# Decoder trunk on one core: products of the convolution in pairs of slots, three kinds of rows read from PSUM, softmax weights scaled on ScalarE and mixed a product later

## The chip, the core and the metric

One core of a Trainium2 chip runs the whole trunk for 256 tokens. The metric is the device time of one execution in microseconds (us), median of three runs: 2081.55 us before (2081.02 to 2082.35). Matrix products run on TensorE (PE), element work on VectorE (DVE), ScalarE (ACT) and GpSimd (POOL); SyncE (SP) issues the loads.

## The reference, cut to what matters

```python
# layer 0: Conformer convolution, then MLP.  layer 1: attention, then MLP.  D = 2048, 256 tokens
u = rmsnorm(h) @ w_in + b_in;  a, gate = split(u);  u = a * sigmoid(gate)
u = causal depthwise conv(u, 31 taps) + b_dw
h = h + silu(layernorm(u)) @ w_out + b_out
h = h + relu(rmsnorm(h) @ m_in)**2 @ m_out          # 2048 -> 8192 -> 2048
k, v = split(rmsnorm(h) @ w_kv)                     # 4 key heads; k rotated in 32 of 128 dims
q = rotate(rmsnorm(h) @ w_q)                        # 16 heads
o = softmax mixture of three dilated windows        # 256 keys: one mask of counts, added as logs
h = h + o @ w_o;  h = h + MLP as above;  out = rmsnorm(h)
```

## The kernel before, in words

Tokens lie along the free dimension (256 columns), features along the partitions, so h is 16 tiles of 128x256. Every weight tile is 128x2048 (1 MB, 16 blocks of 128 contraction rows), loaded in the order of use, and split in two: ACT rounds it to `hi` (line 138), DVE or, for the tiles listed in `POOL_LO`, POOL subtracts `lo = raw - hi` (line 140). Activations are split the same way. `product` (lines 189 to 195) makes two matmuls for each block: `hi` times the 512 columns of both parts, and `lo` times the 256 columns of the first. `product3` (208 to 210) makes three matmuls of 256 columns instead, all adding into the same 256 columns, so that no half is left to be joined. `joined` (199, 200) adds the two halves that `product` leaves.

Stage 1, the convolution layer, goes over 16 channel tiles c. Each has two products (`pa`, `pg`; eight of the 32 tiles are multiplied unsplit by line 214), then a sigmoid and the gated `u` (411, 412), then `conv`: of the 31 taps ACT writes 11, and after POOL has added pairs of them three more, into slots of `prod` buffers (318, 326); DVE does the other 17 taps itself (339 to 344) and sums the slots with two reductions over eight and six slots (350). A slot is 256 adjacent numbers, so the reduction reads numbers that lie 1024 bytes apart. Tile 15 gives 18 of its taps to PE as products with diagonal matrices (309). PE adds up a provisional mean over the first ten tiles (433), which is copied to `shift` in SBUF (436); DVE subtracts it from every tile (`center`, 376), ACT squares, PE sums columns (236). From these come the LayerNorm's factor and offset, spread over all partitions in PSUM (247) and copied to SBUF (459). DVE applies them (475, 476), ACT applies silu (478), and `split_into` (220, 221) makes the operand of the next product. `project` starts with four weight tiles at once (16 blocks in `steps`), so PE can begin with the first of these operands.

After the MLP come k and v, then 16 query products, two heads to a pair p. `rotate` (576 to 579) shuffles 32 partitions into `sh` and mixes them with the tables `ropes`. `scores` makes the scaled and masked scores, the maximum, the exponentials with their sums (648), the reciprocals (650) and the scaled weights (653). `flip` transposes them on PE (663 to 666), `mix` multiplies by v (678, 679). The order by program: after the product of an even head `scores(p-1)` and `mix(p-2)`, after an odd one `flip(p-1)`; the last of them stand among the first blocks of the projection by w_o. The scheduler that builds the program draws each engine's order ahead of time from this order and from its own estimate of times; at run time each engine goes through its list in order.

At the end line 721 multiplies the 16 tiles of h by the row of the final norm, and five transfers store them.

Of the kernel before, what the change touches and what calls it, by code (L numbers as in the profile page):

```python
# [18 lines left out]
P = 128  # L19
# [28 lines left out]
POOL_LO = (set(range(36)) - {28}) | set(range(183, 202, 2))  # L48
# [13 lines left out]
def decoder_kernel(ctx, tc, xT, vec, rope, mask, w_in, w_out, w_k, w_v, w_q, w_o, m_in, m_out, out):  # L62
# [220 lines left out]
    with ExitStack() as s1:  # L283
# [16 lines left out]
        def conv(c, u):  # L300
# [13 lines left out]

            def scaled(buf, slots):
                nonlocal j
                for i in slots:
                    nc.scalar.activation(out=buf[:, i, :], in_=u[:, j:j + T], func=AF.Copy, scale=tap(c, j))  # L318
                    j += 1

            for n, m in pieces:
                buf = prodp.tile([P, SLOTS, T], F32, name="prod")
                scaled(buf, range(carry, carry + n))
                if m:
                    room = slice(carry + m, carry + 2 * m)
                    nc.gpsimd.tensor_tensor(out=buf[:, carry:carry + m, :], in0=buf[:, carry:carry + m, :],
                                            in1=buf[:, room, :], op=ALU.add)
                    refills.append((buf, range(SLOTS)[room]))
# [6 lines left out]
            for i, j in enumerate(range(j, TAPS)):  # L335
# [7 lines left out]
                else:  # L343
                    nc.vector.scalar_tensor_tensor(out=a if j < TAPS - 2 else last[:, i % 2, :], in0=x,  # L344
# [3 lines left out]
            for i, (buf, n) in enumerate(bufs):  # L348
                dst = bufs[i + 1][0][:, 0, :] if i + 1 < len(bufs) else v_of(c)
                nc.vector.tensor_reduce(out=dst, in_=buf[:, :n, :].rearrange("p j t -> p t j"), axis=AX.X, op=ALU.add)  # L350
# [40 lines left out]
        for c in range(KT):  # L391
# [38 lines left out]
            if 2 <= c <= SHIFT + 1:  # L430
                if pmean is None:
                    pmean = ps_tile()
                nc.tensor.matmul(pmean[:, :T], lhsT=ones_d, rhs=v_of(c - 2), start=c == 2, stop=c == SHIFT + 1)
            if c == SHIFT + 1:
                shift = up.tile([P, T], F32, name="shift")
                nc.scalar.activation(out=shift, in_=pmean[:, :T], func=AF.Copy, scale=KT / SHIFT)
# [19 lines left out]
        norm = act_tile(F32)  # L456
        norm_ps = pb.rearrange("p (i t) -> p i t", i=2)
        for i in range(2):
            nc.scalar.copy(out=norm[:, i, :], in_=pb[:, i * T:(i + 1) * T])
# [12 lines left out]
    for c in range(KT):  # L472
        z = tmp()
        n = norm if c else norm_ps
        nc.vector.tensor_tensor(out=z, in0=v_of(c), in1=n[:, 0, :], op=ALU.mult)
        nc.vector.tensor_tensor(out=z, in0=z, in1=n[:, 1, :], op=ALU.add)
        s = tmp()
# [95 lines left out]
    def rotate(src):  # L573

        sh = tp.tile([ROT, T], F32, name="sh", tag="t")
        nc.vector.stream_shuffle(sh, src[0:ROT, :], [(i + ROT // 2) % ROT for i in range(ROT)])
        nc.vector.tensor_tensor(out=sh, in0=sh, in1=ropes[:, 1, :], op=ALU.mult)  # L577
        nc.vector.tensor_tensor(out=src[0:ROT, :], in0=src[0:ROT, :], in1=ropes[:, 0, :], op=ALU.mult)
        nc.vector.tensor_tensor(out=src[0:ROT, :], in0=src[0:ROT, :], in1=sh, op=ALU.add)
# [6 lines left out]
    for g in range(NKV):  # L586
# [5 lines left out]
        else:  # L592
            if rb is None:
                rb = rms_kv.rows()
            while waiting:
# [3 lines left out]
                rotate(ks[:, i, :])  # L599
# [27 lines left out]
    def scores(p):  # L627
# [7 lines left out]
        for b in (1, 0):  # L635
# [15 lines left out]
            for j in range(2):  # L651
                i = 2 * b + j
                nc.vector.tensor_scalar(out=pr[:, j, :n], in0=pr[:, j, :n], scalar1=rl[:, i:i + 1], scalar2=None,
                                        op0=ALU.mult)
# [30 lines left out]
    for i in range(NH):  # L685
# [4 lines left out]
        product(ps, take(), acts, range(KT))  # L690
        q = q_of[p][:, i % 2, :]
        joined(q, ps)
        rotate(q)
        if i % 2 == 0:
            if p >= 1:
                scores(p - 1)
            if p >= 2:
                mix(p - 2)
        elif p >= 1:
            flip(p - 1)  # L700
# [3 lines left out]
    for k, do in ((11, lambda: mix(NP - 1)), (7, lambda: flip(NP - 1)), (4, lambda: mix(NP - 2)), (2, lambda: scores(NP - 1))):  # L704
# [82 lines left out]
```

## Time and profile before

| | |
|---|---|
| median of 3 runs | 2081.55 us |
| the profiled execution, its own time | 2082.01 us |
| span of its instructions | 2080.2 us |
| PE busy, loads of weights | 2016.3 us (97%), 1776.2 us |
| DVE, ACT, POOL busy | 1354.6, 979.7, 212.9 us |
| stage 1 (first matmul of the projection by w_out) | ends at 268.84 us |
| attention (first scores to the MLP) | about 1142 to 1283 us |

A span is read from the span's start. Matmuls are pipelined and their ends are modelled, so PE counts as busy for some 0.2 us after it could have begun the next; its work is better read from the distance between starts. A time in brackets behind a row is the idle time just before it and what ended it.

### The profile page before, as it was taken

The page shows a single profiled execution, that of the slowest core. Times are in us where ns is not written, and L with a number is a line of the kernel's source. Part 1 is how long each engine was busy: PE and PEld are TensorE (multiplying, and loading weights), DVE is VectorE, ACT ScalarE, POOL GpSimd, SP SyncE. Part 2 cuts the span into 40 slices and gives each one's busy share as a digit, 9 for nine tenths or more (in the row PEclk, how much of TensorE's full clock was granted, in tenths as well). Part 3 has the DMA queues.
Part 4 walks back from the last instruction along what each step waited for, and adds up shares of the span by engine and source line. Part 5 has one row for each costly group of instructions (what it writes and reads, how often), then busy time and mean ns, then how long its engine had stood idle before and what let it go on. Part 6 is the DMA issues. An engine that isn't in the chain of part 4 may idle for free.

```text
span 2080.2 us, 28137 instructions
## 1 busy us (share of the span) xinstructions
PE 2016.3 (97%) x11702; PEld 1776.2 (85%) x11702; DVE 1354.6 (65%) x1807; ACT 979.7 (47%) x1324; POOL 212.9 (10%) x83
## 2 busy tenths in 40 slices
PE   8989889999999999999999899999999999999997
PEld 7888778888888888888888787888888888888886
DVE  7999977556556556555676786755555555655664
ACT  4676664443453354345454444444345335434442
POOL 2687600000000000000003220000000000000000
PEclk9999899999999999999999999999999999999999
DMA  7344325555555555555555334555555555555552
GB/s 290 130 154 159 105 108 185 187 185 193 187 196 184 185 194 186 186 191 193 182 183 186 122 138 142 191 188 184 187 192 192 182 189 195 183 186 196 185 185 78
DMA packets 51583, 367.39 MB, mean 177 GB/s; under 512 B 5856, under 2 KB 5856, under 8 KB 7552
## 3 DMA queue, kind: packets, MB, share of 16 engines
q1 hardware_dynamic: 51312, 365.60, 50.7%
q8 instruction: 91, 1.49, 0.3%
q14 instruction: 36, 0.29, 0.0%
q10 hardware_dynamic: 144, 0.01, 0.0%
HBM read 363.49 MB, written 2.10 MB: 176 GB/s over the span
## 4 chain that ended last, share of the span: by engine, by line
PE 50%; issue 35%; DVE 12%; ACT 2%; POOL 0%; DVEq 0%; POOLq 0%; ACTq 0%
PE ps L194 31%; PE ps L195 16%; DVE ps L344 3%; DVE prod L350 2%; DVE act L350 2%; DVE sh L577 1%; ACT hi L138 1%; ACT prod L318 1%; DVE prod L344 1%; DVE act L376 0%; PE ps L639 0%; DVE act L221 0%; PE ps L612 0%; PE ps L611 0%; PE ps L610 0%
## 5 line engine op out<-in xcount | busy, mean ns | idle before, releaser
L194 PE MATMUL ps<-act,hi 128*128 128x512 f32 x4928 | 1731.3, 395 | 4.9 <-DVE act L221 4.1
L195 PE MATMUL ps<-act,lo 128*128 128x256 f32 x4928 | 1381.7, 281 | 4.1 <-DVE lo L140 4.1
L194 PEld LDWEIGHTS ps<-act,hi 128*128 128x128 f32 x4928 | 925.1, 188 | 217.7 <-DVE act L221 4.8
L138 ACT CAST hi<-raw 128x2048 fp32r<-128x2048 f32 x336 | 641.0, 1910 | 853.5 <-PE ps L194 691.4
L140 DVE TENSOR_TENSOR lo<-raw,hi 128x2048 fp32r<-128x2048 f32 x298 | 682.9, 2291 | 431.6 <-ACT hi L138 428.6
L195 PEld LDWEIGHTS ps<-act,lo 128*128 128x128 f32 x4928 | 933.3, 189 | 6.6 <-DVE lo L140 4.7
L494 DVE TENSOR_TENSOR h<-ps,h 128x256 f32<-128x256 f32 x288 | 119.6, 424 | 193.4 <-PE ps L195 189.2
L140 POOL TENSOR_TENSOR lo<-raw,hi 128x2048 fp32r<-128x2048 f32 x38 | 175.0, 4608 | 129.7 <-ACT hi L138 103.6
L241 POOL TENSOR_TENSOR rc<-ms,neg_half 128x2 f32<-128x2 f32 x5 | 3.6, 730 | 1666.3 <-DVE ms L270 1666.3
L318 ACT ACTIVATE prod<-u,vecs 128x256 f32<-128x256 f32 x217 | 90.5, 497 | 58.1 <-DVE u L412 53.8
L208 PE MATMUL ps<-act,hi 128*128 128x256 f32 x384 | 113.1, 294 | 0.0
L210 PE MATMUL ps<-act,lo 128*128 128x256 f32 x384 | 111.1, 289 | 0.1
L209 PE MATMUL ps<-act,hi 128*128 128x256 f32 x384 | 110.9, 289 | 0.0
L344 DVE SCALAR_TENSOR_TENSOR ps<-u,vecs,ps 128x256 f32<-128x256 f32 x197 | 79.6, 483 | 0.0
L208 PEld LDWEIGHTS ps<-act,hi 128*128 128x128 f32 x384 | 76.0, 198 | 0.3
L209 PEld LDWEIGHTS ps<-act,hi 128*128 128x128 f32 x384 | 76.0, 198 | 0.3
L210 PEld LDWEIGHTS ps<-act,lo 128*128 128x128 f32 x384 | 75.9, 198 | 0.3 <-POOL lo L140 0.3
L536 ACT ACTIVATE t<-t 128x256 f32<-128x256 f32 x128 | 52.5, 410 | 42.5 <-DVE t L534 42.5
L221 DVE TENSOR_TENSOR act<-t,act 128x256 fp32r<-128x256 f32 x144 | 60.1, 417 | 8.3 <-ACT act L220 8.3
L214 PE MATMUL ps<-act,raw 128*128 128x256 f32 x256 | 57.8, 386 | 6.7 <-DMA raw<-in_w_in 6.7
L214 PEld LDWEIGHTS ps<-act,raw 128*128 128x128 f32 x256 | 49.2, 194 | 13.4 <-DVE act L295 6.7
L350 DVE TENSOR_REDUCE prod<-prod 128x256 f32<-128x2048 f32 x15 | 58.2, 3877 | 1.6 <-ACT prod L318 0.5
(113 smaller groups left out, 903.0 us busy)
## 6 DMA issues: line engine op xcount, KB each, us to landing
raw<-in_m_in SPq DMA_DIRECT2D x128, 1024.0 KB, 4.8
raw<-in_m_out SPq DMA_DIRECT2D x128, 1024.0 KB, 4.8
raw<-in_w_in SPq DMA_DIRECT2D x31, 1024.0 KB, 4.9
raw<-in_w_out SPq DMA_DIRECT2D x16, 1024.0 KB, 4.9
raw<-in_w_q SPq DMA_DIRECT2D x16, 1024.0 KB, 4.8
raw<-in_w_o SPq DMA_DIRECT2D x16, 1024.0 KB, 4.9
raw<-in_w_k SPq DMA_DIRECT2D x4, 1024.0 KB, 4.9
raw<-in_w_v SPq DMA_DIRECT2D x4, 1024.0 KB, 4.8
```

The lines of the kernel that those rows point to most:

```text
L138: nc.scalar.copy(out=hi, in_=raw)
L140: eng.tensor_tensor(out=lo, in0=raw, in1=hi.bitcast(F32), op=ALU.subtract)
L194: nc.tensor.matmul(ps, lhsT=wh, rhs=a.rearrange("p i t -> p (i t)"), start=k == 0, stop=False)
L195: nc.tensor.matmul(ps[:, :T], lhsT=wl, rhs=a[:, 0, :], start=False, stop=k == KT - 1)
L208: nc.tensor.matmul(ps, lhsT=wh, rhs=a[:, 0, :], start=k == 0, stop=False)
L209: nc.tensor.matmul(ps, lhsT=wh, rhs=a[:, 1, :], start=False, stop=False)
L210: nc.tensor.matmul(ps, lhsT=wl, rhs=a[:, 0, :], start=False, stop=k == KT - 1)
L214: nc.tensor.matmul(ps, lhsT=w[:, k * P:(k + 1) * P], rhs=act_of(k), start=k == 0, stop=k == KT - 1)
L318: nc.scalar.activation(out=buf[:, i, :], in_=u[:, j:j + T], func=AF.Copy, scale=tap(c, j))
L344: nc.vector.scalar_tensor_tensor(out=a if j < TAPS - 2 else last[:, i % 2, :], in0=x, scalar=tap(c, j), in1=a, op0=ALU.mult, op1=ALU.add)
L350: nc.vector.tensor_reduce(out=dst, in_=buf[:, :n, :].rearrange("p j t -> p t j"), axis=AX.X, op=ALU.add)
L494: nc.vector.tensor_tensor(out=h[:, f, :], in0=half, in1=h[:, f, :], op=ALU.add)
```

## The change

Six edits. (1) The buffers `prod` hold slots in pairs: number t of slots 2j and 2j+1 lie side by side, 8 bytes from one t to the next. ACT, POOL and DVE write and read single slots at that step (POOL's addition of two pairs becomes two instructions), and the reduction runs over pairs. (2) The provisional mean's matrix of ones holds the final factor, and `center` reads the mean from PSUM; the copy 436 is gone. (3) The LayerNorm rows are read from PSUM by all 16 tiles; the two copies 459 are gone; silu writes to PSUM. (4) `rotate` keeps `sh` in PSUM and takes a source and a destination; queries are made by `product3`, copied by ACT and rotated from PSUM, so that `joined` is gone there. (5) The softmax weights are scaled by ACT, not DVE; `flip` and `mix` of a pair come one product later each. (6) Three more `lo` tiles (36 to 38, of w_out) go from DVE to POOL, and the last multiplication is done in 5 wide instructions, not 16.

```diff
-POOL_LO = (set(range(36)) - {28}) | set(range(183, 202, 2))
+POOL_LO = (set(range(39)) - {28}) | set(range(183, 202, 2))
+        ones_s = up.tile([P, P], F32, name="ones_s")
+        nc.gpsimd.memset(ones_s, 1.0 / (SHIFT * P))
...
+            def slot(buf, i):
+                return buf[:, i // 2, :, i % 2]
...
-                    nc.scalar.activation(out=buf[:, i, :], in_=u[:, j:j + T], func=AF.Copy, scale=tap(c, j))
+                    nc.scalar.activation(out=slot(buf, i), in_=u[:, j:j + T], func=AF.Copy, scale=tap(c, j))
...
-                buf = prodp.tile([P, SLOTS, T], F32, name="prod")
+                buf = prodp.tile([P, SLOTS // 2, T, 2], F32, name="prod")
...
-                    nc.gpsimd.tensor_tensor(out=buf[:, carry:carry + m, :], in0=buf[:, carry:carry + m, :],
-                                            in1=buf[:, room, :], op=ALU.add)
+                    for i in range(carry, carry + m):
+                        nc.gpsimd.tensor_tensor(out=slot(buf, i), in0=slot(buf, i), in1=slot(buf, i + m), op=ALU.add)
...
-                nc.vector.tensor_reduce(out=dst, in_=buf[:, :n, :].rearrange("p j t -> p t j"), axis=AX.X, op=ALU.add)
+                nc.vector.tensor_reduce(out=dst, in_=buf[:, :n // 2].rearrange("p j t i -> p t j i"), axis=AX.XY,
+                                        op=ALU.add)
...
-                nc.tensor.matmul(pmean[:, :T], lhsT=ones_d, rhs=v_of(c - 2), start=c == 2, stop=c == SHIFT + 1)
+                nc.tensor.matmul(pmean[:, :T], lhsT=ones_s, rhs=v_of(c - 2), start=c == 2, stop=c == SHIFT + 1)
             if c == SHIFT + 1:
-                shift = up.tile([P, T], F32, name="shift")
-                nc.scalar.activation(out=shift, in_=pmean[:, :T], func=AF.Copy, scale=KT / SHIFT)
+                shift = pmean[:, :T]
...
-        norm = act_tile(F32)
-        norm_ps = pb.rearrange("p (i t) -> p i t", i=2)
-        for i in range(2):
-            nc.scalar.copy(out=norm[:, i, :], in_=pb[:, i * T:(i + 1) * T])
+        norm = pb.rearrange("p (i t) -> p i t", i=2)
...
-        s = tmp()
+        s = ps_tile()[:, :T]
         nc.scalar.activation(out=s, in_=z, func=AF.Silu, scale=col("lng", c), bias=col("lnb", c))
...
-    def rotate(src):
-        sh = tp.tile([ROT, T], F32, name="sh", tag="t")
+    def rotate(dst, src):
+        sh = ps_tile()[:ROT, :T]
         nc.vector.stream_shuffle(sh, src[0:ROT, :], [(i + ROT // 2) % ROT for i in range(ROT)])
         nc.vector.tensor_tensor(out=sh, in0=sh, in1=ropes[:, 1, :], op=ALU.mult)
-        nc.vector.tensor_tensor(out=src[0:ROT, :], in0=src[0:ROT, :], in1=ropes[:, 0, :], op=ALU.mult)
-        nc.vector.tensor_tensor(out=src[0:ROT, :], in0=src[0:ROT, :], in1=sh, op=ALU.add)
+        nc.vector.tensor_tensor(out=dst[0:ROT, :], in0=src[0:ROT, :], in1=ropes[:, 0, :], op=ALU.mult)
+        nc.vector.tensor_tensor(out=dst[0:ROT, :], in0=sh, in1=dst[0:ROT, :], op=ALU.add)
...
-                nc.vector.tensor_scalar(out=pr[:, j, :n], in0=pr[:, j, :n], scalar1=rl[:, i:i + 1], scalar2=None,
-                                        op0=ALU.mult)
+                nc.scalar.activation(out=pr[:, j, :n], in_=pr[:, j, :n], func=AF.Copy, scale=rl[:, i:i + 1])
...
-        product(ps, take(), acts, range(KT))
+        product3(ps[:, :T], take(), acts, range(KT))
         q = q_of[p][:, i % 2, :]
-        joined(q, ps)
-        rotate(q)
+        nc.scalar.copy(out=q, in_=ps[:, :T])
+        rotate(q, ps[:, :T])
         if i % 2 == 0:
+            if p >= 2:
+                flip(p - 2)
             if p >= 1:
                 scores(p - 1)
-            if p >= 2:
-                mix(p - 2)
-        elif p >= 1:
-            flip(p - 1)
+        elif p >= 2:
+            mix(p - 2)
...
-    for k, do in ((11, lambda: mix(NP - 1)), (7, lambda: flip(NP - 1)), (4, lambda: mix(NP - 2)), (2, lambda: scores(NP - 1))):
+    for k, do in ((12, lambda: mix(NP - 1)), (9, lambda: flip(NP - 1)), (5, lambda: mix(NP - 2)),
+                  (2, lambda: flip(NP - 2)), (1, lambda: scores(NP - 1))):
...
-        for i in range(f, f + n):
-            nc.vector.tensor_tensor(out=h[:, i, :], in0=h[:, i, :], in1=rb, op=ALU.mult)
+        nc.vector.tensor_tensor(out=h[:, f:f + n, :], in0=h[:, f:f + n, :],
+                                in1=rb.unsqueeze(1).broadcast_to([P, n, T]), op=ALU.mult)
```

## Rows read from the trace of the kernel before

**Rows 1.** Page, part 1: busy us, share of the span, instructions.

```profile
PE 2016.3 (97%) x11702; PEld 1776.2 (85%) x11702; DVE 1354.6 (65%) x1807; ACT 979.7 (47%) x1324; POOL 212.9 (10%) x83
```

**Rows 2.** Waits of PE, whole span: line, releaser, us in total, times, longest.

```profile
PE ps L433 <- DVE act L350: 13.1, 8, 2.8
PE ps L663 <- DVE act L653: 8.0, 2, 7.4
...
PE ps L236 <- ACT t L378: 6.4, 3, 3.4
PE ps L195 <- DVE lo L140: 4.1, 2, 2.3
...
PE ps L236 <- DVE act L376: 3.3, 2, 2.7
PE ps L639 <- DVE act L579: 3.0, 4, 0.8
```

**Rows 3.** Windows: us; busy PE, PEld, DVE, ACT, POOL (instructions); granted clock; DMA.

```profile
220.00:240.00 20.00, 17.84 (x119) 17.64 (x119) 20.00 (x28) 13.13 (x26) 13.60 (x6) 0.80 0.31 106
240.00:260.00 20.00, 17.30 (x77) 15.44 (x77) 20.00 (x27) 11.36 (x24) 9.36 (x4) 0.74 0.31 106
1140.00:1160.00 20.00, 12.63 (x66) 10.83 (x65) 14.79 (x26) 7.49 (x13) 7.59 (x2) 0.83 0.46 157
```

**Rows 4.** Timeline of PE over one steady channel: start, length, line, shapes, wait.

```profile
122.01 0.70 PE L433 MATMUL ps<-act,ones_d 128*128 128x256 f32 x2 [1.71 <-DVE act L350]
...
133.82 0.28 PE L209 MATMUL ps<-act,hi 128*128 128x256 f32 x1
133.94 0.28 PE L210 MATMUL ps<-act,lo 128*128 128x256 f32 x1
135.93 0.70 PE L433 MATMUL ps<-act,ones_d 128*128 128x256 f32 x2 [1.71 <-DVE act L350]
```

**Rows 5.** Groups of DVE, 0 to 300 us: shapes, count, busy us, mean ns, idle.

```profile
L350 DVE TENSOR_REDUCE prod<-prod 128x256 f32<-128x2048 f32 x15 | 58.2, 3877 | 1.6 <-ACT prod L318 0.5
L350 DVE TENSOR_REDUCE act<-prod 128x256 f32<-128x1536 f32 x15 | 43.4, 2896 | 0.4
...
L376 DVE TENSOR_TENSOR act<-act,shift 128x256 f32<-128x256 f32 x16 | 9.9, 661 | 0.0
```

**Rows 6.** Groups of DVE in the attention, 1140 to 1290 us.

```profile
L577 DVE TENSOR_TENSOR sh<-sh,ropes 32x256 f32<-32x256 f32 x15 | 27.6, 1843 | 0.3
...
L645 DVE TENSOR_REDUCE mx<-act 128x2 f32<-128x512 f32 x8 | 5.3, 669 | 0.0
...
L645 DVE TENSOR_REDUCE mx<-act 128x2 f32<-128x256 f32 x8 | 3.2, 402 | 0.0
```

**Rows 7.** Groups: POOL from 0 to 300 us, and line 140 on DVE (page, part 5).

```profile
L140 POOL TENSOR_TENSOR lo<-raw,hi 128x2048 fp32r<-128x2048 f32 x28 | 129.1, 4613 | 23.3 <-ACT hi L138 8.1 <-DVE ps L344 6.2 <-issue 4.7
...
L326 POOL TENSOR_TENSOR prod<-prod 128x256 f32<-128x256 f32 x16 | 14.0, 873 | 31.7 <-ACT prod L318 19.5 <-DVE ps L342 8.4 <-DVE act L376 3.8
...
L140 DVE TENSOR_TENSOR lo<-raw,hi 128x2048 fp32r<-128x2048 f32 x298 | 682.9, 2291 | 431.6 <-ACT hi L138 428.6
```

**Rows 8.** Timeline of PE at the end of stage 1.

```profile
241.49 0.28 PE L210 MATMUL ps<-act,lo 128*128 128x256 f32 x1
...
249.98 10.63 PE L309 MATMUL ps<-u,act 128*128 128x256 f32 x36
...
268.84 0.80 PE L194 MATMUL ps<-act,hi 128*128 128x512 f32 x1 [3.18 <-DVE act L221]
```

**Rows 9.** Groups of ACT, 262 to 270 us.

```profile
L459 ACT COPY act<-ps 128x256 f32<-128x256 f32 x2 | 0.6, 374 | 2.8 <-PE ps L247 2.8
```

**Rows 10.** Timeline of PE inside a product of 512 and 256 columns.

```profile
1251.06 0.39 PE L194 MATMUL ps<-act,hi 128*128 128x512 f32 x1
...
1251.41 0.39 PE L194 MATMUL ps<-act,hi 128*128 128x512 f32 x1
```

**Rows 11.** Groups of DVE, 2060 us to the end.

```profile
L721 DVE TENSOR_TENSOR h<-h,t 128x256 f32<-128x256 f32 x16 | 5.5, 421 | 1.7 <-ACT t L279 1.7
```

More of the change, by code (lines that the diff above doesn't have):

```diff
@@ L343, in conv @@
                 else:
-                    nc.vector.scalar_tensor_tensor(out=a if j < TAPS - 2 else last[:, i % 2, :], in0=x,
+                    nc.vector.scalar_tensor_tensor(out=a if j < TAPS - 2 else slot(last, i % 2), in0=x,
                                                    scalar=tap(c, j), in1=a, op0=ALU.mult, op1=ALU.add)
@@ L348, in conv @@
             for i, (buf, n) in enumerate(bufs):
-                dst = bufs[i + 1][0][:, 0, :] if i + 1 < len(bufs) else v_of(c)
-                nc.vector.tensor_reduce(out=dst, in_=buf[:, :n, :].rearrange("p j t -> p t j"), axis=AX.X, op=ALU.add)
+                dst = slot(bufs[i + 1][0], 0) if i + 1 < len(bufs) else v_of(c)
+                nc.vector.tensor_reduce(out=dst, in_=buf[:, :n // 2].rearrange("p j t i -> p t j i"), axis=AX.XY,
+                                        op=ALU.add)
             if n_pe:
@@ L473, in decoder_kernel @@
         z = tmp()
-        n = norm if c else norm_ps
-        nc.vector.tensor_tensor(out=z, in0=v_of(c), in1=n[:, 0, :], op=ALU.mult)
-        nc.vector.tensor_tensor(out=z, in0=z, in1=n[:, 1, :], op=ALU.add)
-        s = tmp()
+        nc.vector.tensor_tensor(out=z, in0=v_of(c), in1=norm[:, 0, :], op=ALU.mult)
+        nc.vector.tensor_tensor(out=z, in0=z, in1=norm[:, 1, :], op=ALU.add)
+        s = ps_tile()[:, :T]
         nc.scalar.activation(out=s, in_=z, func=AF.Silu, scale=col("lng", c), bias=col("lnb", c))
@@ L598, in decoder_kernel @@
                 nc.vector.tensor_tensor(out=ks[:, i, :], in0=ks[:, i, :], in1=rb, op=ALU.mult)
-                rotate(ks[:, i, :])
+                rotate(ks[:, i, :], ks[:, i, :])
         refill()
```

## The prediction

> **What bounds the kernel now.** I read the busy times first, then the waits of PE, then windows and timelines where those waits lie. PE is busy 97% of the span [rows 1], so over most of the program there is nothing to win but PE's own work, which the change does not cut. What can move is where PE waits. The list of its waits [rows 2] names three places: stage 1 (releasers L350, L378, L376), one wait for `lo` behind each of the two first groups of a projection (L140), and the attention (L653, L579). In stage 1 the reader should see a full DVE: 20.00 of 20 us in both windows from 220 to 260, while ACT has 11 to 13 and PE is down to a clock of 0.80 and 0.74 [rows 3]. One steady channel shows the same on PE: its provisional-mean matmul starts at 122.01 and the next at 135.93, a period of 13.9 us, and the last product before it starts at 133.94, one 0.12 us step from its end; so PE works 12.05 us and loses 1.87 [rows 4]. Stage 1 is bound by DVE, with PE close behind as the next bound. That distance, about 1.8 us a channel, caps what a faster DVE can give in a steady channel.
>
> **Part 1, reductions over pairs.** Two reductions a channel take 3.88 and 2.90 us, 15 of each in these rows (one more stands apart, for tile 15) [rows 5]: the 512 extra numbers cost 0.98 us, 1.92 ns each. Reductions over adjacent numbers cost 0.669 us for 512 and 0.402 us for 256 [rows 6]: 1.04 ns each and 0.135 us fixed. No row shows pairs. The ends by rows: at worst as now, 3.88 and 2.90 (dearer than now is a rival below); at best as adjacent numbers, 0.135 + 2048 x 1.04 = 2.27 and 0.135 + 1536 x 1.04 = 1.73. If each far jump costs the same 0.88 ns extra and every second number is adjacent, the middle, 3.07 and 2.31. I take the best end for the point, since half of the steps are those of the adjacent rows and the point hardly depends on it: DVE's channel falls from 13.9 by 1.61 + 1.17 = 2.8 to 11.1 us at the best end, by 1.4 to 12.5 at the middle, against PE's 12.05.
>
> [...]
>
> POOL is the engine to watch next. A channel has two `lo` of 4.61 us and three additions of one slot, 0.87 each at the mean (the third is new, since the double one becomes two) [rows 7]: 9.23 + 2.62 = 11.8 us, just under PE's 12.05. ACT has 13 of 20 us [rows 3] and room. The writes at a step of 8 bytes have no row; I bound them from nothing to the reduction's extra 0.88 ns a number, 0.23 us for each of ACT's 14 products a channel, 3.2 us, which ACT's idle 7 of 20 us covers; I take nothing.
>
> What PE gets back before its last product (ends 241.6 [rows 8]): the waits for L350, 13.1 us, and for L378, 6.4 [rows 2]; each understated by the modelled end, 1.87 against 1.71 in the channel above, 11 waits, 1.8 us; and clock, 0.80 over one window of 20 us [rows 3], 4.0 us of full speed, on the reading that the idle PE brought it. Sum 25.3. I leave 3.3 us of it to POOL's pace, 0.3 us a channel: 22.0.
>
> **Part 2, the end of stage 1.** From the start of the last product's last matmul to the first of the projection are 268.84 - 241.49 = 27.35 us [rows 8]. DVE is then in arrears, so the diagonal matmuls of tile 15, which need its `u`, begin only at 249.98 and take 10.63 us, partly at a clock of 0.74 [rows 3, 8]. Without arrears: `u` some 1.1 us after the product (two operations near 0.4 us and their hand-overs, an estimate from L645's 0.402 [rows 6]); the diagonals 10.63 x 0.74 = 7.9 us, beside which DVE's 13 taps and its last, now shorter reduction fit; then from the end of the diagonals (260.61) to the projection 8.23 us as now, less the two copies of the LayerNorm rows, 0.65 [rows 9]. Sum 1.1 + 7.9 + 7.6 = 16.6, a gain of 10.7. The centring from PSUM helps DVE here: its mean of 0.66 us [rows 5] against 0.40 for as many numbers [rows 6] holds instances that stood behind POOL; I count it in the arrears, not again. Stage 1 together: -32.7 us.
>
> **Part 3, `lo` 36 to 38 on POOL.** The first `lo` after the four opening tiles is awaited by PE: two waits, 4.1 us in all, one of them here [rows 2]. POOL takes 4.61 where DVE takes 2.29 [rows 7], so this wait grows by 2.3 us; tiles 37 and 38 follow every 4.6 us, under a product's 5.6 (16 x 0.35 [rows 10]). Bounds 0 (POOL starts at once where DVE had residuals to do first) to 4.6. I take +2.3.
>
> **Part 4, attention.** `flip` two products behind its scores no longer meets unfinished weights: the waits for L653, 8.0 us, of which one is 7.4, and the waits of the scores for the rotation, 3.0 us [rows 2], fall away. The latter come from L577: 1.84 us at the mean [rows 6], where 256 numbers in L645 cost 0.40; I read it as DVE standing behind a `lo` of POOL, 4.61 us long [rows 7], in some instances, since both of L577's inputs lie in SBUF as those of the `lo` do. After the change one input is in PSUM. The low clock behind the long wait (0.83 over 20 us, 3.4 us of full speed [rows 3]) half falls in the wait itself; I count 1.5. Against this stands `product3`: three matmuls of 256 at 0.12 us [rows 4] are 0.36 for a block against 0.35 [rows 10], for 256 blocks +2.6. ACT's added scalings are hidden: it is busy 7.5 of 20 us [rows 3]; without that cover, 4 scalings near 0.4 us a pair, eight pairs, 13 us. They wait for DVE's reciprocal, and behind them on ACT stand the `hi` of tiles that PE needs products later; PE waits only if that delay outlasts the tiles split ahead. New PSUM tiles (`sh`, one a head) join eight banks; nine instead of seven are taken per pair of 15 us, each held a few us: I count nothing, bound 1 us a pair, 8 us. Sum -12.5 + 2.6 = -9.9.
>
> [...]
>
> **Part 5, the end.** 16 multiplications, 5.5 us [rows 11], become five over the same numbers; the fixed part of eleven goes, in part overlapped: -0.4.
>
> **The sum**: 2082.0 (profiled execution, 1.8 above its span, 0.46 above the median) - 32.7 + 2.3 - 9.9 - 0.4 = 2041.3, and against the median 2040.8, so 2041.
>
> **Rivals.** *Another engine sets stage 1's pace* (17%): the reduction reaches only the middle (12.5 us a channel), or POOL, with 11.8 us of work and its waits for ACT's slots, stays at 12.8. For it: POOL's margin of 0.25 us. Against: its idle 31.7 us before the additions [rows 7] is waiting for a late `u`. Price 0.5 to 0.8 us in some 14 channels, 7 to 11: about 2050. *The attention gives nothing* (10%): scheduling by estimate puts new waits (PSUM banks, ACT's reciprocal hand-over) where the old were: 2041 + 9.9 = 2051. *The pairs do nothing* (9%): reductions stay at 3.88 and 2.90, DVE still bounds, and stage 1 keeps only the centring (16 x 0.26 = 4.2) and the copies (0.65): 2082.0 - 4.9 + 2.3 - 9.9 - 0.4 = 2069. *Slower* (7%): runs of two with far jumps cost more than eight equal steps. The other gains are 12.9 us in the line above; over 15 channels of 3584 numbers they are used up at 0.24 ns a number more, 2.16 ns. At 2.4 ns a channel costs 1.7 us more, 26 in all: about 2095.
>
> **How the numbers follow.** Forecast 57%, 2041; if all waits of stage 1 go and part 3 costs nothing, 2035, and with the clock fully back some 2030. The range 2030 to 2069 takes in the forecast, both middle rivals and the edge of the third; the slower rival is left out. The measurement can tell about 0.2%, 4 us. Faster by more: 57 + 17 + 10 + most of 9 = 90%; within: 3%; slower: 7%.
>
> **What would show it.** Right: L350 near 2.3 and 1.7 us; the distance between provisional-mean matmuls near 12.1; DVE with gaps in stage 1; the projection starting near 236; L577 near 0.4; no wait at L663 over 1 us; L195 waiting some 4 us near the start of the projection. Wrong: L350 above 3.1 us, POOL without gaps at a period over 12.5, or PE waiting for PSUM in the attention.

## The result, and the profile after

The changed kernel takes 2054.89 us (median of 4 runs, 2054.19 to 2056.42) beside 2081.28 before on the same chip (4 runs, 2080.54 to 2082.35): ratio 0.9874, 95% interval 0.9857 to 0.9891, so 26.4 us less. The forecast was 2041, the range 2030 to 2069. The profiled execution took 2054.33 us, its span is 2052.1.

PE is still the bound. Page, part 1, of the changed kernel (compare [rows 1]):

```profile
PE 2007.8 (98%) x11958; PEld 1780.7 (87%) x11958; DVE 1281.1 (62%) x1745; ACT 988.3 (48%) x1353; POOL 228.3 (11%) x102
```

Its waits are another list. Waits of PE, whole span (line, releaser, us in total, times, longest; compare [rows 2]; the lines moved, L433 is now L439, L663 is L665, L639 is L642):

```profile
PE ps L194 <- DVE act L221: 11.4, 1, 11.4
...
PE ps L194 <- ACT hi L138: 4.1, 3, 2.2
PE ps L195 <- DVE lo L140: 3.6, 2, 2.3
...
PE ps L195 <- POOL lo L140: 1.6, 1, 1.6
...
PE ps L642 <- DVE act L581: 0.4, 1, 0.4
```

The provisional mean, which waited eight times before, and the transposes of the weights, which waited 7.4 us once, are not in the list at all. At its head stands a single wait that nothing in the forecast allowed for: 11.4 us, for the first matmul of the projection by w_out.

To see where each part of the program went, I cut both spans at the same events: the start of the last matmul of stage 1's last product, the first matmul of that projection, the block 512 blocks on (counted by the matmuls of line 194; 256 of them are the projection's, the others the MLP's), the first matmul of the values' product, the last matmul.

| us | before | after | change | forecast |
|---|---|---|---|---|
| start to last product of stage 1 | 241.49 | 212.48 | -29.0 | -22.0 |
| to the first matmul of the projection | 27.35 | 33.25 | +5.9 | -10.7 |
| to the block 512 on | 185.1 | 189.6 | +4.5 | +2.3 |
| to the values' product (MLP) | 649.2 | 649.2 | 0.0 | 0 |
| to the last matmul (attention, MLP) | 967.2 | 957.7 | -9.5 | -9.9 |
| to the end of the span | 9.8 | 9.7 | -0.1 | -0.4 |

The sum is -28.1, the difference of the spans. Two lines are far off, in opposite directions: stage 1 gave more than forecast, its end cost where it should have gained. The rest stands within 2.2 us.

**Stage 1.** Timeline of PE, three successive provisional means (start, length; compare [rows 4]):

```profile
112.77 0.59 PE L439 MATMUL ps<-act,ones_s 128*128 128x256 f32 x2
...
124.71 0.59 PE L439 MATMUL ps<-act,ones_s 128*128 128x256 f32 x2
...
136.65 0.59 PE L439 MATMUL ps<-act,ones_s 128*128 128x256 f32 x2
```

The period is 11.94 us, where it was 13.9, and no row has a wait. Groups of DVE, 0 to 300 us (shapes, count, busy us, mean ns, idle; compare [rows 5]):

```profile
L355 DVE TENSOR_REDUCE prod<-prod 128x256 f32<-128x2048 f32 x15 | 34.3, 2284 | 1.1
L355 DVE TENSOR_REDUCE act<-prod 128x256 f32<-128x1536 f32 x15 | 26.2, 1746 | 0.8 <-ACT prod L323 0.5
...
L382 DVE TENSOR_TENSOR act<-act,ps 128x256 f32<-128x256 f32 x16 | 5.8, 414 | 1.7 <-PE ps L439 1.7
```

The reductions reached the best end of the forecast, 2.28 us against 2.27 and 1.75 against 1.73; 512 numbers more cost 0.54 us, 1.05 ns each, as adjacent ones do [rows 6]. Groups of POOL, same stretch, and windows (us; busy PE, PEld, DVE, ACT, POOL with instructions; granted clock, DMA share, GB/s; compare [rows 3] and [rows 7]):

```profile
L140 POOL TENSOR_TENSOR lo<-raw,hi 128x2048 fp32r<-128x2048 f32 x31 | 143.4, 4632 | 46.0 <-ACT hi L138 42.9 <-DVE act L355 2.8
L332 POOL TENSOR_TENSOR prod<-prod 128x256 f32<-128x256 f32 x46 | 34.8, 776 | 29.9 <-ACT prod L323 23.8 <-DVE ps L347 6.1
```

```profile
60.00:140.00 80.00, 80.00 (x633) 78.79 (x632) 78.51 (x143) 67.37 (x119) 74.46 (x35) 1.00 0.51 180
...
120.00:140.00 20.00, 20.00 (x166) 19.89 (x165) 19.34 (x38) 17.18 (x29) 20.00 (x9) 1.00 0.55 192
...
220.00:240.00 20.00, 12.74 (x57) 10.73 (x57) 10.00 (x26) 6.72 (x13) 0.95 (x2) 0.76 0.21 70
240.00:260.00 20.00, 14.27 (x63) 11.34 (x64) 10.82 (x33) 10.36 (x23) 0.00 (x0) 0.71 0.00 1
```

From 60 to 140 us PE has no idle time and a clock of 1.00; the bound has passed from DVE to PE. In the window from 120 to 140 POOL is full as well and DVE nearly: all three are within a few per cent of each other, so I expect little there from another faster step on DVE.

**The end of stage 1.** Timeline of PE from the last product on:

```profile
215.47 1.72 PE L236 MATMUL ps<-ones_d,t 128*128 128x1 f32 x12 [2.37 <-ACT t L384]
...
219.96 10.23 PE L311 MATMUL ps<-u,act 128*128 128x256 f32 x36
...
245.73 0.79 PE L194 MATMUL ps<-act,hi 128*128 128x512 f32 x1 [11.37 <-DVE act L221]
...
246.72 0.79 PE L194 MATMUL ps<-act,hi 128*128 128x512 f32 x1
...
247.71 0.79 PE L194 MATMUL ps<-act,hi 128*128 128x512 f32 x1
```

and of DVE, the instructions of line 221 that finish the operands of that projection, the first and the tenth to twelfth of 16:

```profile
236.31 0.42 DVE L221 TENSOR_TENSOR act<-ps,act 128x256 fp32r<-128x256 f32 x1
...
245.26 0.41 DVE L221 TENSOR_TENSOR act<-ps,act 128x256 fp32r<-128x256 f32 x1
246.25 0.41 DVE L221 TENSOR_TENSOR act<-ps,act 128x256 fp32r<-128x256 f32 x1
247.25 0.41 DVE L221 TENSOR_TENSOR act<-ps,act 128x256 fp32r<-128x256 f32 x1
```

The operand that the first matmul multiplies is ready at 236.73. PE starts at 245.73, right after DVE has read the tenth (245.26 + 0.41 = 245.67); the next two block starts follow the eleventh (246.66) and the twelfth (247.66) by 0.05 to 0.06 us, and one more at 248.71 the thirteenth (248.65). So the wait is not for an operand. The change lets silu write its result `s` to PSUM, one `ps_tile` for each of the 16 tiles, and line 221 is its last reader. My reading: the four accumulators of the projection were given the places of the tenth to thirteenth `s`, and each opens only when that `s` has been read. The kernel has eight such places (`psp`, line 81); one holds the LayerNorm rows until the end of these 16 tiles, and if the other seven go round, the next four requests after 16 fall on the places of the tenth to thirteenth. PE then starts at a low clock: 0.50 from 245.73 to 249.70, 0.71 over the window from 240 to 260.

### The profile page after: what moved, and what is told of

It reads as the page before. It is cut to its first block, busy times and chain, and to the rows that moved or that the text cites. A ratio compares the mean times of both kernels' runs of the same rounds, so it can differ in the third digit from the quotient of the medians.

```text
span 2052.1 us, 28638 instructions
## 1 busy us (share of the span) xinstructions
PE 2007.8 (98%) x11958; PEld 1780.7 (87%) x11958; DVE 1281.1 (62%) x1745; ACT 988.3 (48%) x1353; POOL 228.3 (11%) x102
## 4 chain that ended last, share of the span: by engine, by line
PE 51%; issue 35%; DVE 2%; ACT 0%; DVEq 0%; POOLq 0%; POOL 0%
PE ps L194 29%; PE ps L195 15%; PE ps L208 1%; PE ps L209 1%; PE ps L210 1%; PE ps L642 0%; DVE lo L140 0%; DVE act L227 0%; PE ps L615 0%; PE ps L614 0%; PE ps L613 0%; PE ps L680 0%; DVE t L262 0%; DVE t L477 0%; DVE t L478 0%
## 5 line engine op out<-in xcount | busy, mean ns | idle before, releaser
L194 PE MATMUL ps<-act,hi 128*128 128x512 f32 x4672 | 1639.1, 395 | 15.4 <-DVE act L221 11.4
L195 PE MATMUL ps<-act,lo 128*128 128x256 f32 x4672 | 1309.7, 281 | 5.3 <-DVE lo L140 3.6
L194 PEld LDWEIGHTS ps<-act,hi 128*128 128x128 f32 x4672 | 876.7, 188 | 219.7 <-DVE act L221 13.1
L195 PEld LDWEIGHTS ps<-act,lo 128*128 128x128 f32 x4672 | 884.6, 189 | 7.7 <-DVE lo L140 4.6
L140 POOL TENSOR_TENSOR lo<-raw,hi 128x2048 fp32r<-128x2048 f32 x41 | 189.4, 4624 | 142.6 <-ACT hi L138 139.5
L208 PE MATMUL ps<-act,hi 128*128 128x256 f32 x640 | 184.6, 288 | 0.0
L209 PE MATMUL ps<-act,hi 128*128 128x256 f32 x640 | 181.0, 283 | 0.0
L209 PEld LDWEIGHTS ps<-act,hi 128*128 128x128 f32 x640 | 122.5, 191 | 0.5
L208 PEld LDWEIGHTS ps<-act,hi 128*128 128x128 f32 x640 | 122.2, 191 | 0.5
L323 ACT ACTIVATE prod<-u,vecs 128x256 f32<-128x256 f32 x217 | 92.4, 517 | 21.3 <-DVE u L418 13.7
L221 DVE TENSOR_TENSOR act<-t,act 128x256 fp32r<-128x256 f32 x128 | 53.3, 416 | 7.4 <-ACT act L220 7.4
L200 DVE TENSOR_TENSOR t<-ps,t 128x256 f32<-128x256 f32 x128 | 53.5, 418 | 1.6 <-ACT t L199 1.6
```

Of the source, the lines that this page charges most:

```text
L140: eng.tensor_tensor(out=lo, in0=raw, in1=hi.bitcast(F32), op=ALU.subtract)
L194: nc.tensor.matmul(ps, lhsT=wh, rhs=a.rearrange("p i t -> p (i t)"), start=k == 0, stop=False)
L195: nc.tensor.matmul(ps[:, :T], lhsT=wl, rhs=a[:, 0, :], start=False, stop=k == KT - 1)
L200: nc.vector.tensor_tensor(out=dst, in0=ps[:, :T], in1=dst, op=ALU.add)
L208: nc.tensor.matmul(ps, lhsT=wh, rhs=a[:, 0, :], start=k == 0, stop=False)
L209: nc.tensor.matmul(ps, lhsT=wh, rhs=a[:, 1, :], start=False, stop=False)
```

## Experiments

The table has each with the same cuts, taken from its one profiled execution; "last product" and "projection" are starts in us, "gap" is their distance, "values to last" the stretch from the values' product to the last matmul. Without a range a time is that of one run.

| kernel | time, us | last product | projection | gap | to the block 512 on | values to last |
|---|---|---|---|---|---|---|
| before | 2081.3 to 2082.4 | 241.49 | 268.84 | 27.4 | 185.1 | 967.2 |
| after | 2054.89 (2054.19 to 2056.42) | 212.48 | 245.73 | 33.3 | 189.6 | 957.7 |
| s_sbuf | 2046.45 (2044.64 to 2047.18) | 212.62 | 237.09 | 24.5 | 188.9 | 957.8 |
| s_ring | 2048.55 (2047.05 to 2049.19) | 212.65 | 236.95 | 24.3 | 188.4 | 960.8 |
| slots_apart | 2082.69 | 242.29 | 273.88 | 31.6 | 189.9 | 957.8 |
| pairs_alone | 2059.18 | 220.54 | 246.22 | 25.7 | 184.0 | 968.1 |
| ssb_lo36 | 2045.51 (2040.94 to 2046.77) | 212.60 | 238.64 | 26.0 | 186.8 | 960.6 |
| ssb_diag | 2045.80 (2044.73 to 2046.63) | 212.93 | 237.31 | 24.4 | 190.5 | 957.9 |
| ssb_lo36_qj | 2070.26 (2068.45 to 2070.50) | 212.74 | 238.81 | 26.1 | 186.9 | 984.3 |
| ssb_qsb | 2064.20 (2063.86 to 2064.54) | 212.76 | 237.19 | 24.4 | 189.4 | 976.7 |
| sh_sbuf | 2057.36 | 212.79 | 247.67 | 34.9 | 189.9 | 958.7 |
| flip_early | 2064.02 | 212.79 | 246.16 | 33.4 | 189.2 | 967.7 |

**The wait of 11.4 us: `s` out of PSUM, and `s` in three places of it.** The theory is the one above; the rival is that a silu, its split, or the LayerNorm rows now read from PSUM are slower. `s_sbuf` puts `s` where it was before:

```diff
-        s = ps_tile()[:, :T]
+        s = tmp()
```

> The changed kernel with one line as before: the result of silu goes to SBUF again. Theory 1 (the first four accumulators of the projection get the PSUM banks of the 10th to 13th silu tiles, so TensorE may not start before those are read): the 11.4 us wait before the first matmul of the projection shrinks to about 2.5 us, it starts near 236.8 us instead of 245.7, and the time is about 2044 us. Theory 2 (the first operand itself is late, through writing silu to PSUM or the order of VectorE): the wait stays near 11 us and the time near 2054 if it is the order, or shrinks only by what silu loses in length (0.57 against 0.60 us) if it is the write.

`s_ring` leaves it in PSUM, in three tiles taken once and used in turn:

```diff
+    ring = [ps_tile() for _ in range(3)]
...
-        s = ps_tile()[:, :T]
+        s = ring[c % 3][:, :T]
```

> The changed kernel, silu still to PSUM, but to three banks that are taken once before the loop and used in turn, so that four banks stay for the accumulators. Theory 1 (banks): as with silu in SBUF, start near 236.8 us and about 2044 us in all. Theory 2 (the write to PSUM or VectorE's order delays the first operand): no gain, about 2054 us.

Both start the projection 8.6 to 8.8 us earlier; ratios to before 0.9828 (0.9812 to 0.9845) and 0.9836 (0.9822 to 0.9851). Timeline of PE in `s_sbuf`:

```profile
212.62 0.28 PE L210 MATMUL ps<-act,lo 128*128 128x256 f32 x1
...
215.61 1.72 PE L236 MATMUL ps<-ones_d,t 128*128 128x1 f32 x12 [2.37 <-ACT t L384]
...
220.59 9.72 PE L311 MATMUL ps<-u,act 128*128 128x256 f32 x36
230.15 0.50 PE L236 MATMUL ps<-ones_d,act 128*128 128x1 f32 x4
...
237.09 0.79 PE L194 MATMUL ps<-act,hi 128*128 128x512 f32 x1 [2.56 <-DVE act L221]
```

The wait is 2.56 us in place of 11.37, and the next blocks start 0.80 and then 0.64 us apart (237.89, 238.53, 239.17), where after the change the first four stood 0.99 us apart. Since `s_ring` keeps silu writing and line 221 reading PSUM and still starts at 236.95, it is not the memory that cost 8.8 us but which places of it were handed out: the theory is shown. `s_ring` loses 3 us again in the attention (960.8), which its edit doesn't touch: ACT and DVE have another order there than in `s_sbuf`, and PE waits 3.7 us once for a `hi` of ACT, 2.2 in `s_sbuf`. `ssb_lo36` below has ACT's order of `s_ring` and 960.6; `ssb_diag` and `slots_apart`, with ACT's order of `s_sbuf`, have 957.9 and 957.8. Besides, four executions of one kernel, `ssb_lo36`, lie between 2040.94 and 2046.77. So a difference of some 3 us between two of these kernels is not to be put down to the edit alone.

**Is it the pairs?** `slots_apart` is the changed kernel with the old layout of the slots; `pairs_alone` is the kernel before with the new layout and nothing else.

```diff
-                return buf[:, i // 2, :, i % 2]
+                return buf[:, i, :]
...
-                buf = prodp.tile([P, SLOTS // 2, T, 2], F32, name="prod")
+                buf = prodp.tile([P, SLOTS, T], F32, name="prod")
...
-                nc.vector.tensor_reduce(out=dst, in_=buf[:, :n // 2].rearrange("p j t i -> p t j i"), axis=AX.XY,
+                nc.vector.tensor_reduce(out=dst, in_=buf[:, :n, :].rearrange("p j t -> p t j"), axis=AX.X,
```

> The changed kernel with the layout of the product slots as before (256 numbers of one slot side by side, reduction at steps of 1024 bytes), all else changed. If the pairs carry the gain of stage 1: reductions 3.9 and 2.9 us again, the distance of the provisional-mean matmuls back to about 13.9 us from 12.2, VectorE full, and the last product of stage 1 ends near 236 us instead of 212.6; time about 2075 us. If the centring from PSUM or POOL's order carried it: last product below 225 us, time below 2066 us.

> The kernel before with the slots in pairs and nothing else. If the pairs alone carry the gain: reductions 2.28 and 1.75 us, the last product of stage 1 ends within 3 us of the changed kernel's 212.6; and since silu stays in SBUF, the projection begins within 25 us after it (33 in the changed kernel, 27 before), so that the time is about 2048 to 2053 us, below the changed kernel's 2054.9, although attention keeps its waits. If the other edits of stage 1 are needed: over 2058 us.

Groups of DVE in `slots_apart`, 0 to 300 us, and the head of its waits of PE; then a group of DVE in `pairs_alone`:

```profile
L355 DVE TENSOR_REDUCE prod<-prod 128x256 f32<-128x2048 f32 x15 | 58.1, 3874 | 1.5 <-ACT hi L138 0.5
L355 DVE TENSOR_REDUCE act<-prod 128x256 f32<-128x1536 f32 x15 | 43.5, 2898 | 0.2
```

```profile
PE ps L439 <- DVE act L355: 13.6, 9, 2.0
PE ps L194 <- DVE act L221: 11.4, 1, 11.4
```

```profile
L380 DVE TENSOR_TENSOR act<-act,shift 128x256 f32<-128x256 f32 x16 | 22.4, 1440 | 0.1
```

With the old layout the reductions take 3.87 and 2.90 us, the waits of the mean are back (13.6 us in nine) and the last product starts at 242.29, later than the 236 that I expected: the other edits give stage 1 nothing as long as DVE is the bound there. The pairs alone bring 21.0 us (241.49 to 220.54), the whole change 29.0, so the second branch of that expectation came: the rest needs another edit. What the change has besides in stage 1 is the mean in PSUM: in `pairs_alone` the 16 subtractions take 1.44 us at the mean, against 0.41 after, 16.6 us of DVE from 163.8 us on. Six of them begin beside a `lo` of POOL, and each of the six ends 0.28 us after it, the longest after 4.85 us; in the kernel before one did (4.20 us; the mean was 0.66 [rows 5]). In that part PE waits 4.2 us for the squares of a centred tile (L236 for L382) and then runs for 6.8 us at a clock of 0.50; that makes 7.6 of the 8.1 us between the two kernels. That it is the mean is found by elimination: no run has the whole change with the mean in SBUF.

**Part 3, `lo` 36 to 38.** `ssb_lo36` is `s_sbuf` with these three tiles back on DVE.

```diff
-POOL_LO = (set(range(39)) - {28}) | set(range(183, 202, 2))
+POOL_LO = (set(range(36)) - {28}) | set(range(183, 202, 2))
```

> Silu to SBUF as in s_sbuf, and the three lo tiles 36 to 38 back on VectorE. Theory A (the move to POOL costs on the path: 4.6 us for 2.3, and VectorE's operations with two SBUF inputs stand behind it for over 4 us each): from the projection's start to its 512th block of the MLP falls from 188.9 us (s_sbuf) to about 184.5, and the time from 2046 to about 2042 us. The forecast's size would be 2.3 us less, about 2044. Theory B (the longer stretch comes from the lower clock at its start alone): no change, 2046.

The 512 blocks take 186.8 us against 188.9: the part costs 2.1 us, the forecast was 2.3. (All kernels of the table with these three `lo` on POOL have 188.4 to 190.5, the others 184.0 to 186.9.) The total stays that of `s_sbuf` (2045.51 and 2046.45, overlapping ranges), as the gap and the attention are 1.6 and 2.8 us longer, neither through the edit: in the gap PE is at half clock (0.50) for 10.2 us from 216.2, in `s_sbuf` for 6.8 from 217.2, and in the attention the order differs, as said. In the 512 blocks PE waits 2.0 us for a `hi` of ACT in both kernels, and in `s_sbuf` 1.6 us more, once, for POOL's `lo`; the clock over the first 60 us is 0.91 there against 0.93, some 1.2 us. The two are enough for the price. DVE is held up as well. In `s_sbuf` its instructions run like this while POOL makes the three `lo` from 261.60 to 275.61:

```profile
262.30 4.12 DVE L227 SCALAR_TENSOR_TENSOR act<-h,vecs,act 128x256 fp32r<-128x256 f32 x1
...
266.67 4.45 DVE L227 SCALAR_TENSOR_TENSOR act<-h,vecs,act 128x256 fp32r<-128x256 f32 x1
271.04 4.84 DVE L262 TENSOR_TENSOR t<-t 128x256 f32<-128x256 f32 x1
275.81 0.47 DVE L227 SCALAR_TENSOR_TENSOR act<-h,vecs,act 128x256 fp32r<-128x256 f32 x1
```

Each lasts until 0.28 us after POOL's current `lo`; the next of its kind, after POOL, takes 0.47. But PE has no further wait in the 512 blocks of `s_sbuf`, so I can't show that this costs PE anything here.

**The gap that is left.** In `s_sbuf` it is 24.5 us where the forecast had 16.6. One suspect was the order on PE, where the column sums of five tiles stand ahead of the diagonal matmuls. `ssb_diag` queues most of them behind:

```diff
+        diag_end = []
...
-                    nc.tensor.matmul(pd[:, :T], lhsT=diags[c][i], rhs=u[:, i:i + T],
-                                     start=i == 0, stop=i == n_pe - 1)
+                    diag_end[:] = [nc.tensor.matmul(pd[:, :T], lhsT=diags[c][i], rhs=u[:, i:i + T],
+                                                    start=i == 0, stop=i == n_pe - 1)]
...
-        statistics()
+        with tc.issue_after(diag_end[0].ins):
+            statistics()
```

> s_sbuf, with the column sums of the last statistics queued on PE behind the 18 diagonal products of tile 15 (all but those of one tile), instead of ahead of them. Theory A, part of the 8 us by which the gap between the last product and the projection of s_sbuf (24.47) exceeds the forecast (16.6) is PE's order: the diagonals, ready with u at 216.3, start at 216.5 to 217.5 in place of 220.59; they end some 4 us earlier, the ten pairs of column sums that now follow them take 2 to 3 us more, beside DVE's last two operations, so the projection starts 1.5 to 4 us earlier, at 233 to 235.6, and the time is 2042.5 to 2045 if the attention keeps its length. Theory B, the order does not matter, since the chain through DVE and the column sums of tile 15 ends last anyway: projection at 236.5 to 237.5, 2046.5. In both, u still comes 3.4 us after the product, since its sigmoid stands behind a hi on ACT.

Timeline of PE:

```profile
216.81 11.04 PE L312 MATMUL ps<-u,act 128*128 128x256 f32 x36
227.69 0.95 PE L236 MATMUL ps<-ones_d,t 128*128 128x1 f32 x8
...
237.31 0.79 PE L194 MATMUL ps<-act,hi 128*128 128x512 f32 x1 [2.55 <-DVE act L221]
```

The diagonals start 3.8 us earlier and end 2.5 us earlier, and the projection starts as before: theory A falls. The sums now follow and run until 232.2 (232.4 in `s_sbuf`); they are work of PE that lies on this path in either order. The diagonals took 10.9 us from start to start against 9.6, as the clock is 0.50 for the first 6.1 us of them, in `s_sbuf` for 3.5; so part of the gain also went into the low clock.

**The attention.** `sh_sbuf` takes the one buffer `sh` back to SBUF, `flip_early` the old order of `flip` and `mix`:

```diff
-        sh = ps_tile()[:ROT, :T]
+        sh = tp.tile([ROT, T], F32, name="sh", tag="t")
```

> The changed kernel with the shuffled rows of the rotation in SBUF again, all else changed. Theory A (PSUM is what ended the waits of the scores): the multiplication of the shuffled rows takes 1.8 us at the mean again and scores wait for the rotation some 3 us in all; time about 2058. Theory B (the order, flip in front of the scores, gives the slack): the multiplication is long again, but the scores wait less than 1 us in all and the time stays within 1 us of 2055.

```diff
-            if p >= 2:
-                flip(p - 2)
             if p >= 1:
                 scores(p - 1)
-        elif p >= 2:
-            mix(p - 2)
+            if p >= 2:
+                mix(p - 2)
+        elif p >= 1:
+            flip(p - 1)
...
-    for k, do in ((12, lambda: mix(NP - 1)), (9, lambda: flip(NP - 1)), (5, lambda: mix(NP - 2)),
-                  (2, lambda: flip(NP - 2)), (1, lambda: scores(NP - 1))):
+    for k, do in ((11, lambda: mix(NP - 1)), (7, lambda: flip(NP - 1)), (4, lambda: mix(NP - 2)), (2, lambda: scores(NP - 1))):
```

> The changed kernel with flip and mix in the order of before, all else changed (queries by product3, rotation through PSUM, weights scaled on ScalarE). Theory A (the later order ended the wait of the first transposes): that wait of 7 us is back, with a low clock behind it, and the time is about 2063. Rival: scaling on ScalarE and the free VectorE alone shorten the softmax, so that the wait is below 4 us and the time below 2060.

Group of DVE in the attention, after and then `sh_sbuf`; last, waits of PE of `flip_early`:

```profile
L580 DVE TENSOR_TENSOR ps<-ps,ropes 32x256 f32<-32x256 f32 x15 | 6.1, 410 | 0.0
```

```profile
L580 DVE TENSOR_TENSOR sh<-sh,ropes 32x256 f32<-32x256 f32 x15 | 29.6, 1970 | 0.0
```

```profile
PE ps L665 <- ACT act L656: 8.6, 7, 2.1
```

With `sh` in SBUF its multiplication takes 1.97 us at the mean again (3.2 to 4.0 in the second head of seven pairs, 0.40 otherwise) and the scores wait 2.5 us in six pieces (L642 for L582), but the stretch is only 1 us longer, 958.7: most of DVE's delay is covered. The order of `flip` is worth 10 us (967.7), all of the part's gain. The waits for unfinished weights come back as forecast in size, 8.6 us against 8.0 [rows 2], though in seven pieces instead of one long one and a short one.

Two kernels ask what `product3` and the rotation from PSUM are worth. `ssb_lo36_qj` (on top of `ssb_lo36`) makes queries by `product` and `joined` again and rotates the copy in SBUF; `ssb_qsb` (on top of `s_sbuf`) keeps `product3` and only rotates from the copy:

```diff
-        product3(ps[:, :T], take(), acts, range(KT))
+        product(ps, take(), acts, range(KT))
...
-        nc.scalar.copy(out=q, in_=ps[:, :T])
-        rotate(q, ps[:, :T])
+        joined(q, ps)
+        rotate(q, q)
```

> As ssb_lo36, and the queries made by the two-matmul product again, joined by ScalarE and VectorE and rotated from SBUF (the shuffled rows stay in PSUM). If product3 costs what the rows gave (0.01 us for a block, 256 blocks): 2.6 us faster than ssb_lo36, about 2040 us. Rival: the rotation's second multiplication has two SBUF inputs again and stands behind POOL, the scores wait for it, and the gain is eaten: equal to ssb_lo36 or up to 3 us slower.

```diff
-        rotate(q, ps[:, :T])
+        rotate(q, q)
```

> s_sbuf, with the query's rotation reading the copy q in SBUF instead of PSUM; product3, ACT's copy and sh in PSUM stay. Theory A, the 23.7 us that ssb_lo36_qj lost are the rotation's operation with two SBUF inputs, standing behind POOL's lo: L581 at 1.8 us at the mean instead of 0.41, waits of the scores for DVE, and 15 to 24 us more from the first product of k and v to the last matmul (957.8 in s_sbuf), so 2061 to 2070. Theory B, they were the two additions of joined: L581 may be long but the distance stays within 4 us of 957.8, 2046 to 2050.

Group of DVE from 1070 to 1240 us in `ssb_qsb` and its first wait of PE; then the first wait of `ssb_lo36_qj`:

```profile
L581 DVE TENSOR_TENSOR act<-act,ropes 32x256 f32<-32x256 f32 x16 | 30.4, 1899 | 0.0
```

```profile
PE ps L642 <- DVE act L582: 14.0, 8, 3.0
```

```profile
PE ps L642 <- DVE act L582: 14.5, 6, 3.9
```

From the values' product to the last matmul `ssb_lo36_qj` loses 23.7 us against `ssb_lo36`, where I had expected a gain of 2.6 or a loss of at most 3; `ssb_qsb` loses 18.9 against `s_sbuf`, with only the rotation's source moved and all matmuls as in the change. So it is the rotation's reading that counts: one operation in the second head of seven pairs takes 3.8 us instead of 0.40 (1.90 at the mean over all heads), and the scores wait 14 us. The other 4.8 us of `ssb_lo36_qj` are what `joined` and `product` cost beyond that, at most, with the scatter of 3 us named above. In the kernel before this rotation also read SBUF, but `sh` took the delay: L577 had 1.84 us at the mean [rows 6] and L578, behind it, 0.41.

`sh_sbuf` with one slow operation loses 1 us, `ssb_qsb` with one loses 19. The traces show why. Here is the same pair in both, first `sh_sbuf`, then `ssb_qsb`: POOL's `lo`, the slow operation of the second head, the scores:

```profile
1166.50 4.62 POOL L140 TENSOR_TENSOR lo<-raw,hi 128x2048 fp32r<-128x2048 f32 x1 [10.87 <-ACT hi L138]
...
1168.19 3.20 DVE L580 TENSOR_TENSOR sh<-sh,ropes 32x256 f32<-32x256 f32 x1
...
1172.11 0.92 PE L642 MATMUL ps<-ks,act 128*128 128x256 f32 x4 [0.51 <-DVE act L582]
```

```profile
1159.84 4.53 POOL L140 TENSOR_TENSOR lo<-raw,hi 128x2048 fp32r<-128x2048 f32 x1 [13.39 <-ACT hi L138]
...
1160.85 3.80 DVE L581 TENSOR_TENSOR act<-act,ropes 32x256 f32<-32x256 f32 x1
...
1165.24 1.11 PE L642 MATMUL ps<-ks,act 128*128 128x256 f32 x6 [2.97 <-DVE act L582]
```

Either operation ends 0.27 to 0.28 us after POOL's `lo`. In this pair and the next three the scores are reached 7.8 us after the last matmul of the second head's product. In `ssb_qsb` ACT has the order that it has in `s_sbuf`, the rotation starts 4.7 to 6.2 us after that matmul, when ACT has made its copy, and ends at 9.7 to 11.2. In `sh_sbuf` ACT's order is another, the rotation starts at 3.4 to 4.5 and ends at 8.5 to 9.1. By these rows it is how late ACT's copy comes that sets what the slow operation costs, and not which of the four it is. What `sh` in PSUM is worth under the change's own order on ACT no run shows.

## Why the prediction was right, and where it was not

The time lies in the range and its sign was right; the forecast itself is 13 us too low (2041.3 against 2054.33, the same kind of execution), and the time lies in the part of the range that was meant for rivals which did not come. By the table of cuts: +16.6 from part 2, +2.2 from part 3, +0.4 from attention, +0.3 from part 5, +0.4 in what lies around the span, less 7.0 that stage 1 gave beyond the forecast.

**Part 1 held.** The reductions came out at the best end, and `slots_apart` and `pairs_alone` show that they carry the gain. The period is 11.94 (forecast 12.1). The 3.3 us left to POOL were not needed: PE has no gap from 60 to 140 us although POOL is busy for 74.5 of the 80. My price of POOL's additions was off: the mean of 0.87 us in [rows 7] holds one of 2.94 among 15 of 0.72 to 0.75, and after the change the three of a channel take 0.61, 0.85 and 0.85 us. ACT's writes at a step of 8 bytes, taken at nothing, cost 0.02 us each (L323 517 ns at the mean, L318 before 497). The clock was mis-sized: I counted one window [rows 3], 4.0 us, but the windows before the last product of the kernel before, at 0.98 over 80 us, 0.99 over 80 and 0.81 over 21.4, add to 1.6 + 0.8 + 4.1 = 6.5. After, it is 1.00 in all of them. 3.3 and 2.5 make 5.8 of the 7.0; of the other 1.2 the first wait of the program gives 0.3 (6.4 against 6.7 us), the rest I can't place.

That pairs reach the pace of adjacent numbers was an estimate; the runs show 2284 ns in pairs and 3877 with the numbers 1024 bytes apart, and not why.

**Part 2 failed, in two steps.** The first is one that I left out. I asked about PSUM for the attention ("eight banks; nine instead of seven are taken") and not for `s`, the other tile that the change moves there: 16 more `ps_tile` just ahead of four accumulators that are all opened at once. That was 8.8 us. The kernel has eight such places (`psp`, line 81); `s_ring` against after shows that an unlucky share of them costs 8.8 us here.

The second is the working of the 16.6 us. Read again, [rows 8] leaves out rows of PE between 241.49 and 249.98, which I took as waiting for `u`. They are work. Timeline of PE before, the first and the last of these rows:

```profile
244.47 0.60 PE L236 MATMUL ps<-ones_d,act 128*128 128x1 f32 x4 [2.70 <-DVE act L376]
...
249.12 0.99 PE L236 MATMUL ps<-ones_d,act 128*128 128x1 f32 x4
```

Only 2.70 of the 8.49 us are a wait; 5.5 are column sums, and they are there after the change too: 4.2 us, from `u` (215.95 + 0.48 = 216.4) to the diagonals at 220.59 in `s_sbuf`. Of the other terms, `u` comes 3.8 us after the last product's last matmul starts, not 1.1, as its sigmoid stands on ACT behind a `hi` of 1.9 us, 212.94 to 214.74; the diagonals take 9.6, not 7.9, since the clock is still at 0.50 for the first 3.5 us of them; the rest 6.9, not 7.6. 4.2 + 2.7 + 1.7 - 0.7 = 7.9, and 16.6 + 7.9 = 24.5, the gap of `s_sbuf`. A faster DVE removed its arrears there, but work of PE stood behind them that the waits before had hidden in part.

**Part 3 held in size**, 2.1 against 2.3. The +4.5 of the table holds more than this part. By the traces PE's waits in the 512 blocks are 3.9 us in three pieces after and 1.8 in one before, 2.2 us more; the clock over the first 60 us is 0.92 against 0.94, 1.2 us; and the first four blocks, which open with the places of `s`, take 3.8 us against 2.7 in `s_sbuf`, 1.1 us.

**Part 4 held in sum**, 9.5 against 9.9, partly by luck, since its terms did so only in part. The order of `flip` and `mix` gives 10 us, which I had priced at 8.0 + 1.5. `sh` in PSUM, priced at 3.0, gives 1 in `sh_sbuf`, with another order on ACT. `product3` costs about what I put down: its blocks start 0.360 us apart, those of before 0.351, which is 2.3 us for 256 against 2.6. But it is also what leaves a sum in PSUM that can be rotated from there; without that reading 18.9 us are lost (`ssb_qsb`). I had looked at a form of matmul by its own length and not at who reads its output.

**The signs named ahead.** The reductions, the 11.94 us, L577 (now L580) at 0.41 and no wait over 1 us at L663 came as written. The projection starts at 245.73, not near 236; without the wait for PSUM, in `s_sbuf`, at 237.09, where the 7.0 us more of stage 1 and the 7.9 us more of the gap cancel. Of the 4 us of L195 near the projection's start 2.9 came, 1.6 for POOL's `lo` and, 14 us later, 1.3 for one of DVE. The gaps on DVE are small: 19.34 of 20 us are busy from 120 to 140, 55.7 of 60 from 140 to 200.

**The rivals.** That another engine would set stage 1's pace, that the attention gives nothing, that the pairs do nothing: none came. The measured time is near 2050, the price of the first two, but for neither's reason.

## What to carry to other kernels

A tile that is moved to PSUM took a place here from what was opened next (8.8 us), so ask of each such move which long-lived accumulators follow it, and give short-lived tiles a few fixed places of their own (three in `s_ring`). Where a stretch between two rows is to shrink, list every instruction inside it on the engine that is late: work that stood in the shadow of a wait stayed here when the wait went (4.2 us of column sums). A short operation of DVE with both inputs in SBUF that began beside a `lo` of POOL was held here until that one had ended (4.12 to 4.84 us in `s_sbuf`); with one input in PSUM it took 0.41 to 0.42 (L382 after). The best of these kernels, `s_sbuf` and its relatives, are at 2045.5 to 2046.5 us, 8 to 9 below the change and 36 below the kernel before.

## What the runs showed of the hardware

A reduction over numbers 1024 bytes apart cost 1.92 ns a number (L350 before), in pairs of adjacent numbers 1.05 (L355 after): as little as if all were adjacent (1.04 [rows 6]). Short operations of DVE with both inputs in SBUF that began beside a `lo` of POOL ended 0.27 to 0.29 us after it: 0.41 to 0.47 us became 4.12 to 4.84 in `s_sbuf`, 3.8 for L581 in `ssb_qsb`, up to 4.85 for L380 in `pairs_alone`; the subtraction with one input in PSUM (L382 after) took 0.41 to 0.42 in the 14 of 16 that began beside a `lo`. Additions on POOL at a step of 8 bytes (L332) took 0.60 to 0.63 us where both inputs lie in the same pairs of slots and 0.84 to 0.89 where they lie in different pairs; with adjacent numbers 15 of the 16 additions of one slot in the kernel before (L326) took 0.72 to 0.75.
